# Three changes of queue order in the feed-forward part of a hybrid encoder block

## The chip, the cores and the metric

The kernel runs on one core of a Trainium2 chip. The metric is the device time of one execution in microseconds (us); the median of several executions is compared. A core has a matrix engine (TensorE, PE in the profile), a vector engine (VectorE, DVE), an activation engine (ScalarE, ACT), a general engine (GpSimd, POOL) and a sync engine (SyncE, SP) that here only issues transfers. Each engine works through its own queue of instructions in order, and engines wait for each other by semaphores. Transfers between DRAM and the on-chip memory (DMA) are issued from the queues of SP, ACT or POOL.

## The reference

One residual layer on 2048 rows of 1024 float32 values. Attention and a recurrent mixer come first; the change lies in the last line, the feed-forward network (FFN):

```python
x = x + rms_norm(merged @ w_out, post_mix_g)
hf = rms_norm(x, pre_ffn_g)
u = square(relu(hf @ w_up)) @ w_down      # 1024 -> 4096 -> 1024
x = x + rms_norm(u, post_ffn_g)
```

Every product is to float32 accuracy: each operand is split into a high part (rounded to the matrix engine's float32r) and a low part (operand minus high part), and three matmuls high·high, low·high and high·low are summed.

## The kernel before

**Stages.** The rows are four groups of 512. The mixing of each group comes first (up to about 2050 us of the span) and isn't touched. The FFN then runs over two halves of two groups (1024 rows): `phase_up(0)`, `phase_down(0)`, `phase_up(1)`, `phase_down(1)`. Each of the two products of the FFN is done by a Strassen-Winograd scheme: seven block products in place of eight, on sums and differences of operand blocks.

**Splitting.** `split` (L69) casts to the high part on ACT (L70) and subtracts on DVE to get the low part (L71). A product can begin when the high parts are there and goes on to the low parts one matmul later.

**phase_up.** It runs 16 turns `i`. A turn loads two row blocks of `w_up` (`raw0`, `raw1`, four buffers, L1211), forms the sums `s12` and `s4` on DVE (L1260 to L1266), casts A11/A12 (tile `a1`), S1/S2 (`s12`), S3/A22 (`s3`) and S4 (`s4`), and TensorE runs products with the tiles t2, t3, t1, b22 and t4. The results go through add, relu and square (`hidden`, L1222 to L1224) into the tile X, and from there by GpSimd's DMA to DRAM (`xd`, L1227). For the first eight turns (`early`) the product with `a1` was done ahead, in a loop at the start of the phase, while the operands t2 to t4 were still loading; so only turns 8 to 15 cast `a1` within the turn (L1257). `b1` (tiles bh and bl, "first half" of the activations) is loaded and split by `first_half` (L1161), with `split_here` (L1156), a split in place; for half 1 this is done during `phase_down(0)`, as part of the generator `beside`.

**phase_down.** Seven products, named "1", "6", "7", "5", "4", "3" and "2" in the order in which they run, of eight steps `f` each. A step takes a block of the activations (`xraw`, L1322) and one of `w_down` or its combinations (`wdraw`, L1325 or L1327), each split into the tile `fop`, and runs 24 matmuls, six for each of four row tiles. The loads share four buffers, so the load of one step's block goes out when a low half two steps earlier is done. After a product's last step `gather` adds each row tile's bank into `u` (L1360). After "4" the four tiles of the second group are complete, after "2" those of the first; `final` (L1362) closes a tile: sums of squares on ACT (L1371), multiplication by the gain on DVE (L1372), statistics on GpSimd (L1374, L107), `u * r + x` on DVE (L1378), with `x` loaded by SP into one of two buffers (x1r, L1366), and the store to the output by SP (L1381).

**What sets the order.** The code is written in one order; a scheduler then places each engine's instructions by its own estimate of when their inputs are ready, and the engines keep the order that it made. `queue_behind(a, b)` (L84) adds a dependence without a semaphore, which only tells the scheduler that instruction `a` stands later than `b`. `queue_behind(self.relu, high)` in `operands` (L1331) is one that was there.

Of the kernel before, what the change touches and what calls it, by code (L numbers as in the profile page):

```python
# [24 lines left out]
G = 512  # L25
# [17 lines left out]
def advance(steps, n=None):  # L43

    while n is None or n > 0:
        if next(steps, steps) is steps:
            return
        n = n and n - 1


class Block:
# [1103 lines left out]

    def split_here(self, hi, lo):  # L1156

        self.nc.scalar.copy(hi, lo.bitcast(F32))
        self.nc.vector.tensor_tensor(lo, lo.bitcast(F32), hi.bitcast(F32), ALU.subtract)

    def first_half(self, g, bp):  # L1161

        bh, bl = self.b1 = [bp.tile([P, KB, G], F32R, tag="b" + x, name="b" + x) for x in "hl"]
        for k in range(0, KB, 2):
            ks = slice(k, k + 2)
            self.nc.sync.dma_start(bl[:, ks].bitcast(F32), self.ht[g][:, ks])
            self.split_here(bh[:, ks], bl[:, ks])
            yield

    def phase_up(self, half, zp, rp, cb, pn, early):  # L1170
# [6 lines left out]
        with ExitStack() as ctx:  # L1177
# [36 lines left out]
            def parts(src, tag, n):  # L1214
                pool = sp if tag in ("a1", "s12") else late
                hl = [pool.tile([P, n, P], F32R, tag=tag + x, name=tag + x) for x in "hl"]
                self.split(*hl, src)
                return [[x[:, i : i + KH] for x in hl] for i in range(0, n, KH)]

            def hidden(dst, src, x):  # L1220
# [29 lines left out]
            for i in range(FF // P // 2):  # L1250
                raw0, raw1 = load(2 * i), load(2 * i + 1)
                if i < early:
                    x = cb.tile([P, G], F32, tag="c", name="x11")
                    nc.sync.dma_start(x, self.xd[0][i // 2][:, i % 2])
                (a11, a12), (a21, a22) = ((x[:, lo4], x[:, hi4]) for x in (raw0, raw1))
                if i >= early:
                    A11, A12 = parts(raw0, "a1", KB)  # L1257
                s12 = up.tile([P, KB, P], F32, tag="s1", name="s12")
                s4 = up.tile([P, KH, P], F32, tag="s4", name="s4")
                nc.vector.tensor_tensor(s12[:, lo4], a21, a22, ALU.add)  # L1260
                nc.vector.tensor_tensor(s12[:, hi4], s12[:, lo4], a11, ALU.subtract)
                S1, S2 = parts(s12, "s12", KB)

                nc.vector.tensor_tensor(a21, a11, a21, ALU.subtract)
                S3, A22 = parts(raw1, "s3", KB)
                nc.vector.tensor_tensor(s4, a12, s12[:, hi4], ALU.subtract)  # L1266
                (S4,) = parts(s4, "s4", KH)

                if i < early:
                    p1 = z[:, i]  # L1270
                else:
                    p1 = up.tile([P, G], F32, tag="p1", name="p1")
                    nc.scalar.copy(p1, product(A11, B11, self.pd, "d"))
                    x = first(i, p1)
                q = up.tile([P, G], F32, tag="q", name="q")
                w = up.tile([P, G], F32, tag="w", name="w")
                nc.vector.tensor_tensor(q, p1, product(S2, T["t2"], pn, "dn"), ALU.add)
                if last is not None:
                    sums(*last)
                nc.vector.tensor_tensor(w, q, product(S3, T["t3"], pn, "dn"), ALU.add)  # L1280
                ps = product(S1, T["t1"], pn, "dn")
                hidden(X[:, 1], w, ps)
                keep(2, i, X[:, 1])
                nc.vector.tensor_tensor(q, q, ps, ALU.add)
                hidden(X[:, 2], q, product(S4, T["b22"], pn, "dn"))
                hidden(X[:, 0], w, product(A22, T["t4"], pn, "dn"))
                keep(1, i, X[:, 0])
                last = i, x
            sums(*last)

    def phase_down(self, half, zp, rp, cb, pn, beside_of):
# [4 lines left out]
        with ExitStack() as ctx:  # L1296
# [21 lines left out]
            def operands(s):  # L1318
                q, x, w, f = steps[s]
                t = (zp, ring)[s % 2].tile([P, 4, 2, G], F32R, tag=("z", "op")[s % 2], name="fop")  # L1320
                xr = rp.tile([P, 2, G], F32, tag="raw", name="xraw")
                nc.sync.dma_start(xr, self.xd[x][f])  # L1322
                wr = rp.tile([P, 2, G], F32, tag="raw", name="wdraw")
                if isinstance(w, int):
                    nc.sync.dma_start(wr, self.wd[w][f])  # L1325
                else:
                    nc.sync.dma_start(wr, wrows[w[0]][:, 2 * f : 2 * f + 2, w[1]])  # L1327
                self.split(t[:, 0], t[:, 1], xr)
                high = self.split(t[:, 2], t[:, 3], wr)
                if s == 1:  # L1330
                    self.queue_behind(self.relu, high)  # L1331
                return t

            def bank():
# [27 lines left out]
            def final(t):  # L1362
                th = t // GT
                g, ts = gs[th], slice((t % GT) * P, (t % GT + 1) * P)
                x = op.tile([P, D], F32, tag="x", name="x1r")
                nc.sync.dma_start(x, self.x1[g][ts])  # L1366
                ssq = op.tile([P, 2], F32, tag="ssq", bufs=4, name="ssqu")
                for n in (1, 0):
                    ns = slice(n * G, (n + 1) * G)
                    sq = cb.tile([P, G], F32, tag="c", name="squ")  # L1370
                    nc.scalar.activation(sq, u[t][:, ns], AF.Square, accum_out=ssq[:, n : n + 1])  # L1371
                    nc.vector.tensor_tensor(u[t][:, ns], u[t][:, ns], gt[:, ns], ALU.mult)  # L1372
                    yield
                nc.gpsimd.tensor_tensor(ssq[:, 0:1], ssq[:, 0:1], ssq[:, 1:2], ALU.add)  # L1374
                r = self.rstd(op, ssq[:, 0:1], 1.0 / D, RMS_EPS)
                for n in range(2):
                    ns = slice(n * G, (n + 1) * G)
                    nc.vector.scalar_tensor_tensor(  # L1378
                        u[t][:, ns], u[t][:, ns], r, x[:, ns], op0=ALU.mult, op1=ALU.add
                    )  # L1380
                nc.sync.dma_start(self.out[g * G + ts.start : g * G + ts.stop], u[t])  # L1381
                yield

            NS = len(steps)
# [3 lines left out]
            for s, (q, x, w, f) in enumerate(steps):  # L1388
# [12 lines left out]
                for t in range(GT):  # L1401
                    down(ps[t], t, o, f == 0, f == NF // 4 - 1)
                    if f == NF // 4 - 1:
                        gather(q, t, ps[t])
                        if q == "4":
                            advance(ends[GT + t])
                        elif q == "3":
                            advance(ends[t], 1)
                        elif q == "2":
                            advance(ends[t])  # L1410
                if f % 3 == 1 or f == NF // 4 - 1:
                    advance(beside, 1)
            advance(beside)
# [95 lines left out]
```

## Time and profile before

| | us |
|---|---|
| median of 3 executions (lowest to highest) | 3300.28 (3299.59 to 3302.99) |
| the profiled execution | 3302.74 |
| its span, first to last instruction | 3301.0 |
| TensorE busy / DVE / ACT / POOL | 3189.4 / 2245.6 / 1570.8 / 595.8 |
| phase_up(0), about | 2050 to 2361 |
| phase_down(0), about | 2361 to 2673 |
| phase_up(1), about | 2673 to 2985 |
| phase_down(1), about | 2985 to 3290 |

The profile is of one execution. A timeline row gives the start, the length, the engine, the line and operation, what is written and read, how many such instructions are merged in the row, and in brackets how long the engine stood idle before it and what ended that wait. A row of the list of waits gives the waiting engine and line, what it waited for, and then the total in us, the count and the longest. In a group row the number after the bar is the busy time in us, then the mean length in ns, then the idle time before. In a row of a table by windows the columns are start and end, length, busy us (and count) of PE, PEld (the weight loads), DVE, ACT and POOL, then the granted TensorE clock (1.00 is full), the DMA engines' busy share and GB/s. Successive matmuls overlap: a row's length is longer than the distance between starts. SPq rows are the issue of a DMA, not its transfer.

### The profile page before, as it was taken

The page shows a single profiled execution, that of the slowest core. Times are in us where ns is not written, and L with a number is a line of the kernel's source. Part 1 is how long each engine was busy: PE and PEld are TensorE (multiplying, and loading weights), DVE is VectorE, ACT ScalarE, POOL GpSimd, SP SyncE. Part 2 cuts the span into 40 slices and gives each one's busy share as a digit, 9 for nine tenths or more (in the row PEclk, how much of TensorE's full clock was granted, in tenths as well). Part 3 has the DMA queues.
Part 4 walks back from the last instruction along what each step waited for, and adds up shares of the span by engine and source line. Part 5 has one row for each costly group of instructions (what it writes and reads, how often), then busy time and mean ns, then how long its engine had stood idle before and what let it go on. Part 6 is the DMA issues. An engine that isn't in the chain of part 4 may idle for free. (4 is left out here: it accounts for less than half of the span.)

```text
span 3301.0 us, 49967 instructions
## 1 busy us (share of the span) xinstructions
PE 3189.4 (97%) x18913; PEld 2601.3 (79%) x18913; DVE 2245.6 (68%) x3655; ACT 1570.8 (48%) x2511; POOL 595.8 (18%) x1093
## 2 busy tenths in 40 slices
PE   7999999999999999999999999999999999999998
PEld 5777778778877777878777887878788878888887
DVE  5875766785766875776876775777656667775455
ACT  3434634434744434754444654544543454454343
POOL 2222012222102222111232110122211112220000
PEclk9999999999999999999999999999999999999999
DMA  5335473247564236555326647654787875546665
GB/s 152 90 110 185 129 239 118 81 131 240 170 223 150 87 108 222 189 194 185 96 76 201 200 155 234 231 179 153 248 291 239 285 248 190 170 161 235 193 215 178
DMA packets 432281, 592.53 MB, mean 179 GB/s; under 512 B 25300, under 2 KB 295840, under 8 KB 432040
## 3 DMA queue, kind: packets, MB, share of 16 engines
q1 hardware_dynamic: 375080, 413.14, 40.0%
q0 software_dynamic: 47744, 159.42, 13.1%
q10 hardware_dynamic: 9216, 16.78, 1.4%
q8 instruction: 149, 2.44, 0.3%
q14 instruction: 92, 0.75, 0.1%
HBM read 425.37 MB, written 167.01 MB: 179 GB/s over the span
## 5 line engine op out<-in xcount | busy, mean ns | idle before, releaser
L1345 PE MATMUL ps_dn<-fop 128*128 128x512 f32 x2688 | 611.8, 389 | 2.9 <-DVE fop L71 2.9
L1345 PEld LDWEIGHTS ps_dn<-fop 128*128 128x128 f32 x2688 | 503.9, 188 | 108.9 <-DVE fop L71 4.3
L80 PE MATMUL psd<-hh,whi 128*128 128x512 f32 x1344 | 541.4, 403 | 10.7 <-ACT whi L70 7.0
L80 PE MATMUL psd<-hl,whi 128*128 128x512 f32 x1344 | 542.4, 404 | 0.0
L80 PE MATMUL psd<-hh,wlo 128*128 128x512 f32 x1344 | 538.5, 401 | 2.6 <-DVE wlo L71 2.6
L70 ACT CAST whi<-wraw 128x1024 fp32r<-128x1024 f32 x232 | 243.3, 1049 | 424.1 <-PE psd L80 329.9
L71 DVE TENSOR_TENSOR wlo<-wraw,whi 128x1024 fp32r<-128x1024 f32 x232 | 282.9, 1220 | 165.9 <-ACT whi L70 139.1
L80 PEld LDWEIGHTS psd<-hh,whi 128*128 128x128 f32 x1344 | 255.9, 190 | 62.1 <-ACT whi L70 7.9
L80 PEld LDWEIGHTS psd<-hh,wlo 128*128 128x128 f32 x1344 | 256.1, 191 | 55.9 <-DVE wlo L71 5.1
L80 PEld LDWEIGHTS psd<-hl,whi 128*128 128x128 f32 x1344 | 256.5, 191 | 48.9
L71 DVE TENSOR_TENSOR fop<-xraw,fop 128x1024 fp32r<-128x1024 f32 x112 | 137.0, 1223 | 166.7 <-ACT fop L70 165.9
L70 ACT CAST fop<-xraw 128x1024 fp32r<-128x1024 f32 x112 | 117.8, 1052 | 244.9 <-PE ps_dn L1345 178.5
L1227 POOL DMA_DIRECT2D xd<-X x192 | 103.8, 541 | 394.3 <-ACT X L1224 339.5
L71 DVE TENSOR_TENSOR fop<-wdraw,fop 128x1024 fp32r<-128x1024 f32 x112 | 136.6, 1220 | 26.6 <-ACT fop L70 26.1
L70 ACT CAST fop<-wdraw 128x1024 fp32r<-128x1024 f32 x112 | 117.7, 1051 | 42.8 <-DMA wdraw<-in_w_down_dram 29.8
L903 DVE CUSTOM_DVE_ANT_0 sc<-bias,ps_s 128x640 f32<-128x640 f32 (+4 forms) x128 | 93.8, 732 | 54.0 <-PE ps_pt L914 32.2
L908 ACT ACTIVATE sc<-sc,mn 128x640 f32<-128x640 f32 (+4 forms) x128 | 97.7, 764 | 45.2 <-DVE mn L903 44.8
L70 ACT CAST s12h<-s 128x1024 fp32r<-128x1024 f32 x32 | 33.7, 1054 | 165.0 <-PE ps_u L80 165.0
L80 PE MATMUL ps_p<-yh,whi 128*128 128x512 f32 x256 | 101.3, 405 | 7.5 <-DVE th L1041 3.8
L1070 PE MATMUL ps_o<-whi,mh 128*128 128x512 f32 x256 | 101.6, 397 | 6.1 <-DVE o L1081 6.1
L919 DVE TENSOR_TENSOR PTl<-ps_pt,PTh 128x640 fp32r<-128x640 f32 (+4 forms) x128 | 94.2, 736 | 18.7 <-ACT PTh L918 17.2
L1070 PE MATMUL ps_o<-wlo,mh 128*128 128x512 f32 x256 | 100.6, 393 | 3.2 <-DVE wlo L71 3.2
(368 smaller groups left out, 6826.1 us busy)
## 6 DMA issues: line engine op xcount, KB each, us to landing
wraw<-in_w_in_dram SPq DMA_DIRECT2D x168, 512.0 KB
xraw<-xd SPq DMA_DIRECT2D x112, 512.0 KB
xd<-X POOLq DMA_DIRECT2D x192, 256.0 KB, 5.2
wraw<-in_w_up_dram SPq DMA_DIRECT2D x80, 512.0 KB
wdraw<-wd SPq DMA_DIRECT2D x64, 512.0 KB
wdraw<-in_w_down_dram SPq DMA_DIRECT2D x48, 512.0 KB
gd<-gate ACTq DMA_DIRECT2D x64, 256.0 KB
wd<-cmb POOLq DMA_DIRECT2D x64, 256.0 KB, 3.7
```

What stands on the lines that cost most here:

```text
L70: high = self.nc.scalar.copy(hi, src)
L71: self.nc.vector.tensor_tensor(lo, src, hi.bitcast(F32), ALU.subtract)
L80: mm.append(nc.tensor.matmul(ps, l, r, start=n == 0, stop=n == last).ins)
L903: nc.vector.tensor_tensor_reduce(sc[:, 0:n], bias[:, s0:640], pss[:, c0 : c0 + n], 1.0, 3.0e38, ALU.add, ALU.min, mn,)
L908: nc.scalar.activation(sc[:, 0:n], sc[:, 0:n], AF.Exp, scale=-1.0, bias=mn, accum_out=sm[:, col : col + 1])
L919: nc.vector.tensor_tensor(lv, pst[:, 0:nk], hv.bitcast(F32), ALU.subtract)
L1070: nc.tensor.matmul(ps[t], l[:, k, ts], r[:, k % 2], start=k == 0 and j == 0, stop=k == KB - 1 and j == 2)
L1227: nc.gpsimd.dma_start(self.xd[q][i // 2][:, i % 2], src)
L1345: nc.tensor.matmul(ps, o[:, l, k, sl], o[:, r, k], start=start and n == 0, stop=stop and n == end)
```

## The change

There are three parts.

1. **Casts that need late rows.** In turn 8, the first whose `a1` is cast within the turn, that cast is queued behind the cast of `s3` of turn 7 (`self.cast3`). And the four casts of bh for half 1 are queued behind `self.second`, the cast of the second `fop` operand of `phase_down(0)`.
2. **Closing tiles.** The four tiles that are complete after product "4" are no longer closed right at its last step, all four, but one each at the steps 0 to 3 of product "3", the sixth.
3. **Stores.** In half 0 the eight output tiles are stored from GpSimd's queue, in half 1 from SP's as before.

```diff
     def split_here(self, hi, lo):
-        self.nc.scalar.copy(hi, lo.bitcast(F32))
+        high = self.nc.scalar.copy(hi, lo.bitcast(F32))
         self.nc.vector.tensor_tensor(lo, lo.bitcast(F32), hi.bitcast(F32), ALU.subtract)
+        return high.ins
...
-            self.split_here(bh[:, ks], bl[:, ks])
+            high = self.split_here(bh[:, ks], bl[:, ks])
+            if g:
+                self.queue_behind(high, self.second)
...
-                self.split(*hl, src)
+                self.cast = self.split(*hl, src)
...
                 if i >= early:
+                    behind = self.cast3
                     A11, A12 = parts(raw0, "a1", KB)
+                    if i == early:
+                        self.queue_behind(self.cast, behind)
...
                 S3, A22 = parts(raw1, "s3", KB)
+                self.cast3 = self.cast
...
                 if s == 1:
                     self.queue_behind(self.relu, high)
+                    self.second = high
...
-                nc.sync.dma_start(self.out[g * G + ts.start : g * G + ts.stop], u[t])
+                queue = nc.sync if half else nc.gpsimd
+                queue.dma_start(self.out[g * G + ts.start : g * G + ts.stop], u[t])
...
-                        if q == "4":
-                            advance(ends[GT + t])
-                        elif q == "3":
+                        if q == "3":
                             advance(ends[t], 1)
                         elif q == "2":
                             advance(ends[t])
+                if q == "3" and f < GT:
+                    advance(ends[GT + f])
```

The scheduler turns this into new orders on ACT, DVE, POOL and SP; TensorE's order stays as it was. Three places follow, with the lines of the changed file where the order is the changed one (L1226 and L1227 there are L1223 and L1224 before, L1368 is L1360, L1380 is L1372, L1386 is L1378).

ACT in `phase_up`, turns 6 to 7, before: the cast of `a1` of turn 8 stands right behind the cast of `s12` of turn 6 (X is the tile of the activations).

```order
L70 CAST s12h<-s_21412 128x1024
L70 CAST a1h<-wraw 128x1024
L1223 ACTIVATE X<-X 128x512
L1224 ACTIVATE X<-X 128x512
L70 CAST s4h<-s_21413 128x512
L1223 ACTIVATE X<-X 128x512
L1224 ACTIVATE X<-X 128x512
L70 CAST s3h<-wraw 128x1024
```

And now, from the cast of `s12` of turn 7 on:

```order
L70 CAST s12h<-s_21525 128x1024
L1226 ACTIVATE X<-X 128x512
L1227 ACTIVATE X<-X 128x512
L70 CAST s4h<-s_21526 128x512
L1226 ACTIVATE X<-X 128x512
L1227 ACTIVATE X<-X 128x512
L70 CAST s3h<-wraw 128x1024
L70 CAST a1h<-wraw 128x1024
```

The cast of `a1` has moved by more than one turn, behind the `s3` of turn 7. The same holds in half 1.

ACT at the change from `phase_up(0)` to `phase_down(0)`, before: the four casts of bh stand ahead of the last block's activations and of the casts of the second operand (`fop`).

```order
L1158 CAST bh<-bl 128x1024 x4
L1223 ACTIVATE X<-X 128x512
L1224 ACTIVATE X<-X 128x512
L1223 ACTIVATE X<-X 128x512
L1224 ACTIVATE X<-X 128x512
L70 CAST fop<-xraw 128x1024
L70 CAST fop<-wdraw 128x1024
```

Now:

```order
L1226 ACTIVATE X<-X 128x512
L1227 ACTIVATE X<-X 128x512
L1226 ACTIVATE X<-X 128x512
L1227 ACTIVATE X<-X 128x512
L70 CAST fop<-xraw 128x1024
L70 CAST fop<-wdraw 128x1024
L1226 ACTIVATE X<-X 128x512
L1158 CAST bh<-bl 128x1024
L1227 ACTIVATE X<-X 128x512
L1158 CAST bh<-bl 128x1024
```

The four casts stand behind the second operand's; the other two follow among the casts of the third and fourth operand. DVE's low halves move in the same way. On SP the load of x1r for a closing tile now stands ahead of the loads of operand 4, and a load of xr ahead of half of operand 6's (operands counted from 0).

DVE at the end of product "4" in half 0, before (tiles u_22847 to u_22850 are the four that close; `fop` are the low halves of the steps of product "3"):

```order
L1372 TENSOR_TENSOR u_22849<-u_22849,g_post_24178 128x512 x2
L1378 SCALAR_TENSOR_TENSOR u_22849<-u_22849,rs_r,x1r 128x512 x2
L1360 TENSOR_TENSOR u_22850<-u_22850,ps_dn 128x512
L1372 TENSOR_TENSOR u_22850<-u_22850,g_post_24178 128x512
L71 TENSOR_TENSOR fop<-xraw,fop 128x1024
L1372 TENSOR_TENSOR u_22850<-u_22850,g_post_24178 128x512
L1378 SCALAR_TENSOR_TENSOR u_22850<-u_22850,rs_r,x1r 128x512 x2
L71 TENSOR_TENSOR fop<-wdraw,fop 128x1024
```

Now:

```order
L1386 SCALAR_TENSOR_TENSOR u_22848<-u_22848,rs_r,x1r 128x512 x2
L1368 TENSOR_TENSOR u_22850<-u_22850,ps_dn 128x512
L71 TENSOR_TENSOR fop<-xraw,fop 128x1024
L71 TENSOR_TENSOR fop<-wdraw,fop 128x1024
L71 TENSOR_TENSOR fop<-xraw,fop 128x1024
L71 TENSOR_TENSOR fop<-wdraw,fop 128x1024
L1121 TENSOR_TENSOR cmb<-cmb 128x512
L1380 TENSOR_TENSOR u_22849<-u_22849,g_post_24178 128x512
```

Four low halves, those of steps 2 and 3, now stand ahead of the last steps of the third and fourth tile. SP's loads for steps 4 and 5 no longer stand behind stores, which GpSimd now issues: there each store stands behind its own tile's last step on DVE and ahead of a later tile's statistics.

## The prediction

> **What bounds the kernel now.** I read the page first, then the list of who waited for whom, TensorE (PE) alone, from 1800 us on, since everything up to there is left as it was, then the timelines around each wait.
>
> ```profile
> span 3301.0 us, 49967 instructions
> PE 3189.4 (97%) x18913; PEld 2601.3 (79%) x18913; DVE 2245.6 (68%) x3655; ACT 1570.8 (48%) x2511; POOL 595.8 (18%) x1093
> PE ps_u L80 <- ACT s3h L70: 3.9, 2, 2.1
> PE ps_dn L1345 <- DVE fop L71: 2.9, 3, 1.3
> ```
>
> PE is the bound: 97% of the span. Its order isn't changed, so the change can only close gaps between its matmuls or open new ones. The list names five such gaps (two and three) in the FFN, and all five lie where an edit acts. I measure a gap by when the next matmul starts against when it would have: matmuls of one stream start 0.2267 us apart (from the first row of part B, (5.83 − 0.39) / 24).
>
> **A. The cast of a1 that needs late rows (once in each half).** TensorE's timeline at the first gap, then ScalarE's (ACT), in half 0:
>
> ```profile
> 2179.07 0.39 PE L80 MATMUL ps_u<-t2h,s12l 128*128 128x512 f32 x1
> 2181.60 0.50 PE L80 MATMUL ps_u<-t3h,s3h 128*128 128x512 f32 x1 [2.14 <-ACT s3h L70]
> 2186.60 0.39 PE L80 MATMUL ps_u<-t1h,s12h 128*128 128x512 f32 x1
> ```
> ```profile
> 2171.11 1.06 ACT L70 CAST s12h<-s 128x1024 fp32r<-128x1024 f32 x1 [5.90 <-PE ps_u L80]
> 2176.38 1.05 ACT L70 CAST a1h<-wraw 128x1024 fp32r<-128x1024 f32 x1 [4.21 <-DMA wraw<-in_w_up_dram]
> 2180.51 1.03 ACT L70 CAST s3h<-wraw 128x1024 fp32r<-128x1024 f32 x1
> 2189.31 1.05 ACT L70 CAST s12h<-s 128x1024 fp32r<-128x1024 f32 x1 [6.57 <-PE ps_u L80]
> 2194.75 1.06 ACT L70 CAST s3h<-wraw 128x1024 fp32r<-128x1024 f32 x1
> 2211.29 0.59 ACT L1273 COPY p<-ps_u 128x512 f32<-128x512 f32 x1 [0.68 <-PE ps_u L80]
> ```
>
> The cast of a1 stands behind that of s12 and waits 4.21 us for rows still in flight; s4 and s3 stand behind it. In the next turn, which has no a1, s3 follows s12 by 5.44 us (2194.75 − 2189.31); here by 9.40. With a1 gone from there s3 starts at 2171.11 + 5.44 = 2176.55, and TensorE wants it at 2179.30. The first matmul behind the twelve of t3 should start at 2179.07 + 13 × 0.2267 = 2182.02 and starts at 2186.60: **4.58 us** come off. At its new place, behind the s3 that ends at 2195.8, a1 has 12 us: the product that it feeds ended at 2211.29, so began about 2208.5. Its low half moves along on VectorE (DVE), 1.22 us there in an engine that is idle for 32% of the span; at worst these 1.22 us are paid once in each half.
>
> What is late next? The sums that VectorE forms from the following rows, L1260, which now stand ahead of s4's and s3's low halves. One group tells how late they run over all 32 turns:
>
> ```profile
> L1260 DVE TENSOR_TENSOR s<-wraw 128x512 f32<-128x512 f32 x32 | 22.1, 690 | 2.0 <-DMA wraw<-in_w_up_dram 1.1
> 2180.00:2186.00 6.00, 3.86 (x10) 2.80 (x11) 5.83 (x9) 2.71 (x4) 2.64 (x5) 0.72 0.44 132
> 2804.97 0.39 PE L80 MATMUL ps_u<-t2h,s12l 128*128 128x512 f32 x1
> 2807.09 0.50 PE L80 MATMUL ps_u<-t3h,s3h 128*128 128x512 f32 x1 [1.73 <-ACT s3h L70]
> 2810.77 0.39 PE L80 MATMUL ps_u<-t1h,s12h 128*128 128x512 f32 x1
> ```
>
> 2.0 us in all, so nothing there. In half 1 the same sum is 2810.77 − (2804.97 + 13 × 0.2267) = **2.85 us**. Half 0 loses 1.73 us more because the granted clock was 0.72 from 2180 to 2186 (the window's row); half 1 had full clock behind a gap almost as long, so I take those 1.73 us to come in some executions and not in others. The Trainium skill (TensorE: Matmul & The Clock Gate, Part 1) says that the clock halves after an idle window of about 3.4 us that runs freely, so that the same kernel may or may not be caught. By it no gap of 2.1 us need be caught, and A would be 5.70 in place of 7.43; the trace shows one caught, and the other not.
>
> **B. The casts of bh for half 1.** TensorE, then ScalarE, VectorE and SyncE (SP), at the start of half 0's down phase; then the DMA engines' busy tenths from 2340 to 2400, in slices of 1.5 us, and two groups for the length of one activation and one add (mean ns, before the second bar):
>
> ```profile
> 2360.69 5.83 PE L1345 MATMUL ps_dn<-fop 128*128 128x512 f32 x25
> 2367.78 11.29 PE L1345 MATMUL ps_dn<-fop 128*128 128x512 f32 x48 [1.26 <-DVE fop L71]
> 2379.83 10.97 PE L1345 MATMUL ps_dn<-fop 128*128 128x512 f32 x47 [0.76 <-DVE fop L71]
> ```
> ```profile
> 2357.63 1.05 ACT L1158 CAST bh<-bl 128x1024 fp32r<-128x1024 f32 x1 [0.21 <-DMA bl<-ht]
> 2374.32 1.05 ACT L70 CAST fop<-xraw 128x1024 fp32r<-128x1024 f32 x1 [5.99 <-DMA xraw<-xd]
> 2366.51 1.22 DVE L71 TENSOR_TENSOR fop<-wdraw,fop 128x1024 fp32r<-128x1024 f32 x1
> 2383.34 1.22 DVE L71 TENSOR_TENSOR fop<-wdraw,fop 128x1024 fp32r<-128x1024 f32 x1 [0.76 <-ACT fop L70]
> 2366.61 0.32 SPq L1322 DMA_DIRECT2D xraw<-xd  x1
> DMA  3075899999800059679999999999998968999689
> L1224 ACT ACTIVATE X<-X 128x512 f32<-128x512 f32 x96 | 60.8, 633 | 3.1
> L1238 DVE TENSOR_TENSOR X<-X 128x512 f32<-128x512 f32 x64 | 43.8, 684 | 4.4 <-ACT X L1224 4.2
> ```
>
> TensorE should have gone on at 2360.69 + 25 × 0.2267 = 2366.36: 1.42 lost. Then at 2367.78 + 48 × 0.2267 = 2378.66: 1.17 lost. The four casts wait for bl until 2358.7, and the last block's activations and the second operand's casts stand behind them. Without them those casts hang on TensorE's last products. The last but one has its last start 13 × 0.2267 before 2360.69, and a tail of 0.39: it ends at 2358.1. One add (0.68) and two activations (0.63 each) take it to 2360.1, two casts (1.05) to 2362.2; VectorE meanwhile does four adds to 2362.8 and two low halves (1.22) to 2365.3, in time for 2366.36. So the first loss goes whole.
>
> The second is of another kind: operand 3's load goes out at 2366.61, when operand 1's low half frees its buffer, and its cast waits 5.99 us for it. The load now goes out about 2.8 us earlier; TensorE arrives 2.59 earlier. It is gone if the transfers move along, and stays, together with the first, if the DMA is the limit (ready at 2379.83 either way). The DMA stood empty from 2358 to 2362, so they can mostly move; against it, the load of x1r now stands ahead of operand 4's, and that of xr ahead of half of operand 6's. Ends: 2.59, and −1.0 (the first rival); I take **2.0**, nearer to the end that the empty slices speak for. bh itself is needed 300 us later: nothing. Two of its low halves and an add now lie between operand 1's and 2's on VectorE: operand 2 is ready at 2365.3 + 4 × 1.22 + 0.68 = 2370.9 and wanted at 2366.36 + 24 × 0.2267 = 2371.8. If that cover is gone, what is missing of 0.9 us is paid once.
>
> **C. Closing tiles spread over the sixth product's steps.** TensorE around that product in half 0, and in half 1; VectorE in half 0:
>
> ```profile
> 2559.67 36.20 PE L1345 MATMUL ps_dn<-fop 128*128 128x512 f32 x159
> 2596.81 43.38 PE L1345 MATMUL ps_dn<-fop 128*128 128x512 f32 x190 [0.93 <-DVE fop L71]
> 3149.75 140.01 PE L1345 MATMUL ps_dn<-fop 128*128 128x512 f32 x617
> 2595.53 1.22 DVE L71 TENSOR_TENSOR fop<-wdraw,fop 128x1024 fp32r<-128x1024 f32 x1
> ```
>
> In half 0 one gap: 2596.81 − (2559.67 + 159 × 0.2267) = **1.09 us**, for a low half at 2595.53, queued behind the fourth tile's close. In the new order the low halves of two steps stand right behind the fourth tile's last add, ahead of the third and fourth tile's closes (1.42 us each for their last step alone, L1378 in part D's row), so the one that is late by 1.09 us comes at least 2.8 us earlier and the gap goes. Half 1 has no gap (617 matmuls in one piece): 0. The two closes now stand between the low halves of steps 4, 5 and 6, at least 1.42 us in two steps of 5.4 us each (24 × 0.2267); the rest of each step is the cover, and without it a step would pay these 1.42 us.
>
> **D. First half's stores on GpSimd (POOL).** Eight stores leave SP. The nearest rows are GpSimd's own 512 KB stores (L1445), and the wait that SP's late loads cause at half 1's start:
>
> ```profile
> L1445 POOL DMA_DIRECT2D od<-o x16: 531/534/612, 518.0 to 2051.5; - x16
> 2682.26 0.39 SPq L1211 DMA_DIRECT2D wraw<-in_w_up_dram  x1
> 2681.02 1.22 DVE L71 TENSOR_TENSOR s3l<-wraw,s3h 128x1024 fp32r<-128x1024 f32 x1
> 2690.86 0.50 PE L80 MATMUL ps_u<-bh,a1h 128*128 128x512 f32 x1 [1.25 <-ACT z L1244]
> 2668.11 1.42 DVE L1378 SCALAR_TENSOR_TENSOR u<-u,rs_r,x1r 128x512 f32<-128x512 f32 x2 [1.01 <-POOL rs_r L107]
> 2670.96 0.70 POOL L1374 TENSOR_TENSOR ssqu<-ssqu 128x1 f32<-128x1 f32 x1 [2.88 <-ACT squ L1371]
> ```
>
> Eight times 0.534 is 4.3 us of an engine that is 18% busy. The wait at 2690.86 looks like the gain, but the weight load at 2682.26, ahead of the t loads, waits for s3's low half (2681.02 + 1.22), not for the stores. So **0**; at most the 1.4 us of that wait if s3 moves. The new wait: a store waits for its tile's last VectorE step and holds the next tile's statistics behind it in GpSimd's queue. In the closing tiles that step ends at 2669.53 and the next statistics start at 2670.96: 1.43 us of room against 0.534.
>
> **Sum.** 4.58 + 2.85 + 2.0 + 1.09 = 10.5 us. The profiled execution took 3302.74 us (span 3301.0), so 3292.2 by its own time. It lies 2.46 above the median of the runs, 3300.28: from there 3289.8 if the runs also had the slow clock stretch, 3291.5 if not. I say 3290.5.
>
> **Rivals.**
> - *The DMA takes B back.* The loads don't move, and x1r's 0.5 MB (about 1.7 us at the 311 GB/s below) comes ahead of operand 4, ready 0.7 us ahead of time before (2384.56 against 2385.27): −1.0 in place of 2.0, so about 3293.5. For it: the DMA share.
> ```profile
> 2360.00:2392.00 32.00, 29.99 (x135) 24.16 (x134) 20.32 (x20) 18.46 (x21) 10.29 (x17) 1.00 0.90 311
> ```
> - *A trades one wait for another.* VectorE's L1260 finds its rows as late as a1 did, and half of A comes back: about 3295 to 3297. Against it: 2.0 us in 32 turns.
> - *GpSimd's queue becomes the bound: slower.* If a store holds GpSimd for H us, each of the two stores between closing tiles delays all behind it by H − 1.43, down to s3, the t loads and the gap at 2690.86: 2 × (H − 1.43) us. It outweighs A and B (9.4 us; C is then taken back as well) from H = 6.2; at H = 8 the time is about 3304, at 10 about 3308. Against it: 531 to 612 ns in sixteen cases. The Trainium skill (SBUF — State Buffer, two separate sides) has a rule against this edit: a GpSimd DMA's descriptors can't be written while VectorE holds the shared port, some 0.6 us becoming 3.1; by that figure, an estimate, 2 × 1.67 = 3.3 us come back: about 3294. No GpSimd store here shows it.
>
> **How the numbers follow.** Forecast 0.70 (3288 to 3293), DMA 0.13 (half of it below the mark), A's trade 0.11, GpSimd 0.06 (0.04 of it beyond the mark). A measurement of this kernel can tell about 0.2%, 6.6 us, from no change, so faster means below 3293.7: 0.70 + 0.07 = 0.77; slower means above 3306.9: 0.04; the rest, 0.19, is the same. Range: below, 3290.5 less B whole (0.6), the 1.4 of D and 1.5 for the spread of the runs (3299.59 to 3302.99): 3287; above, the DMA rival and the greater part of A's trade: 3296.
>
> **What would show it.** Right: no wait for s3h at PE; matmul records in one piece over the first 96 of half 0's down phase and over its sixth product; stores on GpSimd of about 0.55 us; the wait near 2690, some 8 us earlier in the span, still there. Wrong: a gap before the s3 products from L1260; operand 3 or 4 waiting for DMA; statistics (L1374) late behind a store.

## The result and the profile after

The changed kernel took 3293.61 us (median of 12 executions, 3290.13 to 3298.61), the kernel before 3303.34 beside it (12 executions, 3299.13 to 3310.88): a ratio of 0.9971, with a 95% interval of 0.9962 to 0.998, so 9.7 us less. Measured again beside other kernels it took 3291.04 against 3302.24: 0.9963 (0.9952 to 0.9975). One execution of a kernel further down (g_post and x1r held) took 11015 us; that kernel's median is of its other five.

The page of its profiled execution (3291.34 us), and TensorE's timeline at the places that the prediction spoke of. The first row is a mark that recurs in every kernel here: the first matmul with t2 in turn 0 of half 0, ahead of everything that differs. Then half 0's down phase, its sixth product, and the start of half 1:

```profile
span 3289.6 us, 49976 instructions
...
PE 3181.5 (97%) x18913; PEld 2599.1 (79%) x18913; DVE 2245.5 (68%) x3655; ACT 1570.2 (48%) x2511; POOL 604.0 (18%) x1101
```
```profile
2092.21 0.50 PE L80 MATMUL ps_u<-t2h,s12h 128*128 128x512 f32 x1 [0.91 <-ACT s12h L70]
...
2353.47 16.48 PE L1353 MATMUL ps_dn<-fop 128*128 128x512 f32 x72
2371.26 0.50 PE L1353 MATMUL ps_dn<-fop 128*128 128x512 f32 x1 [1.31 <-ACT fop L70]
2372.52 11.04 PE L1353 MATMUL ps_dn<-fop 128*128 128x512 f32 x47 [0.76 <-DVE fop L71]
...
2539.74 70.43 PE L1353 MATMUL ps_dn<-fop 128*128 128x512 f32 x310
...
2682.70 0.50 PE L80 MATMUL ps_u<-bh,a1h 128*128 128x512 f32 x1 [1.52 <-ACT z L1247]
```

The mark in the kernel before:

```profile
2094.84 0.50 PE L80 MATMUL ps_u<-t2h,s12h 128*128 128x512 f32 x1 [0.91 <-ACT s12h L70]
```

The mark comes 2.63 us earlier although nothing ahead of it was changed. In the fourteen executions profiled for this document it lies anywhere from 2089.4 to 2096.0 us. So a profile is best read from the mark on: the rest of the FFN took 3301.0 − 2094.84 = 1206.2 us before and 3289.6 − 2092.21 = 1197.4 after, 8.8 us less.

In TensorE's rows the down phase now runs 72 matmuls without a break, so operand 1 is in time, but operand 3 isn't: the 74th matmul should have started at 2353.47 + 73 × 0.2267 = 2370.02 and starts at 2372.52, 2.50 us late. That is what both gaps together cost before (2379.83 − 2360.69 − 16.55 = 2.59). The sixth product is one piece. The wait near 2690 is there, 8 us earlier, as forecast.

ScalarE at the casts of a1, then at operand 3; TensorE in the window in which the clock had fallen to 0.72; SyncE's loads at the start of the down phase; GpSimd at one store between closing tiles, and all stores as a group (ns minimum, median, maximum):

```profile
2168.48 1.05 ACT L70 CAST s12h<-s 128x1024 fp32r<-128x1024 f32 x1 [5.89 <-PE ps_u L80]
...
2173.92 1.05 ACT L70 CAST s3h<-wraw 128x1024 fp32r<-128x1024 f32 x1
...
2187.52 1.05 ACT L70 CAST s3h<-wraw 128x1024 fp32r<-128x1024 f32 x1
2188.48 1.05 ACT L70 CAST a1h<-wraw 128x1024 fp32r<-128x1024 f32 x1
...
2368.05 1.05 ACT L70 CAST fop<-xraw 128x1024 fp32r<-128x1024 f32 x1 [5.98 <-DMA xraw<-xd]
2370.16 1.04 ACT L70 CAST fop<-wdraw 128x1024 fp32r<-128x1024 f32 x1 [1.06 <-DMA wdraw<-in_w_down_dram]
```
```profile
2180.00:2186.00 6.00, 6.00 (x29) 1.00 0.99 325
```
```profile
2353.43 0.33 SPq L116 DMA_DIRECT2D g_post<-in_post_ffn_g_dram  x1
2354.95 0.32 SPq L1090 DMA_DIRECT2D o_prev<-od  x1
2355.36 0.44 SPq L1092 DMA_DIRECT2D xr<-in_x_dram  x1
2356.65 0.32 SPq L1329 DMA_DIRECT2D xraw<-xd  x1
2357.79 0.38 SPq L1334 DMA_DIRECT2D wdraw<-in_w_down_dram  x1
2358.27 0.74 SPq L1374 DMA_DIRECT2D x1r<-x  x1
```
```profile
2661.33 0.62 POOL L1390 DMA_DIRECT2D out_dram<-u  x1 [1.75 <-DVE u L1386]
2662.48 0.69 POOL L1382 TENSOR_TENSOR ssqu<-ssqu 128x1 f32<-128x1 f32 x1 [0.53 <-ACT squ L1379]
...
L1390 POOL DMA_DIRECT2D out_dram<-u x8: 531/620/627, 2576.1 to 2672.3; - x8
```

s3 follows s12 by 5.44 us, a1 stands behind the next s3 and waits for nothing, and TensorE is busy all through 2180 to 2186 at full clock. The store is done before the next statistics could begin: these wait 0.53 us for ScalarE's sum of squares, not for the store. At operand 3 the load (xraw) is issued 3.18 us after the start of the phase (5.92 before), but its cast begins 14.58 us after the start (13.63 before: 2374.32 − 2360.69). In this execution the load left earlier and landed no earlier.

### The profile page after: what moved, and what is told of

It is laid out like the page before. It is cut to its first block, busy times and chain, and to the rows that moved or that the text cites. A ratio compares the mean times of both kernels' runs of the same rounds, so it can differ in the third digit from the quotient of the medians.

```text
span 3289.6 us, 49976 instructions
## 1 busy us (share of the span) xinstructions
PE 3181.5 (97%) x18913; PEld 2599.1 (79%) x18913; DVE 2245.5 (68%) x3655; ACT 1570.2 (48%) x2511; POOL 604.0 (18%) x1101
## 5 line engine op out<-in xcount | busy, mean ns | idle before, releaser
L919 DVE TENSOR_TENSOR PTl<-ps_pt,PTh 128x640 fp32r<-128x640 f32 (+4 forms) x128 | 94.3, 737 | 18.6 <-ACT PTh L918 17.1
```

The lines of the kernel that those rows point to most:

```text
L919: nc.vector.tensor_tensor(lv, pst[:, 0:nk], hv.bitcast(F32), ALU.subtract)
```

## The experiments

Theory: the gain is A, 7.4 us and more where the clock would have fallen, plus C's 1.1; B gives almost nothing, since the transfers issued at the start of the down phase decide when operand 3's rows land; D is nothing. Rivals: A only trades its waits and B and C give the gain; the loads move along and something else in the combined kernel took B; GpSimd's stores cost, or relieve SyncE.

Effects of 1 to 3 us are less than an interval of the medians (about ± 3 to 4 us in five rounds), so the rest of the FFN from the mark to the end of the span is read beside them, one execution each:

| kernel | mark | span | rest of FFN | against before |
|---|---|---|---|---|
| before | 2094.84 | 3301.0 | 1206.2 | |
| a1 edit alone | 2092.06 | 3290.2 | 1198.1 | −8.0 |
| bh edit alone | 2094.41 | 3304.1 | 1209.7 | +3.5 |
| closing tiles alone | 2089.40 | 3296.8 | 1207.4 | +1.2 |
| stores alone | 2089.99 | 3296.8 | 1206.8 | +0.7 |
| changed | 2092.21 | 3289.6 | 1197.4 | −8.8 |
| changed, again | 2092.85 | 3289.9 | 1197.1 | −9.1 |
| changed, old closing tiles | 2095.95 | 3294.2 | 1198.3 | −7.9 |
| changed, x1r held | 2094.55 | 3290.7 | 1196.2 | −10.0 |
| changed, g_post held | 2091.80 | 3287.8 | 1196.0 | −10.2 |
| changed, one more load | 2089.77 | 3285.2 | 1195.4 | −10.7 |
| changed, g_post and x1r held | 2092.51 | 3287.4 | 1194.9 | −11.3 |
| changed, residual held too | 2090.94 | 3285.8 | 1194.9 | −11.3 |
| the same, and z first | 2090.35 | 3284.6 | 1194.3 | −11.9 |

### Each part alone, in the kernel before

**The a1 edit.**

```diff
-                self.split(*hl, src)
+                self.cast = self.split(*hl, src)
...
+                    behind = self.cast3
                     A11, A12 = parts(raw0, "a1", KB)
+                    if i == early:
+                        self.queue_behind(self.cast, behind)
...
                 S3, A22 = parts(raw1, "s3", KB)
+                self.cast3 = self.cast
```

> The kernel before with the a1 edit alone (bh's casts, closing tiles and stores as before). Main theory (the gain is A, plus C's 1.1 us, and B gives 0.2): both waits for s3h are gone from TensorE's list, and 5.7 to 7.4 us of the time with them (ratio about 0.998), the lower figure if the kernel before doesn't run its first gap at the slow clock; the gaps at operands 1 and 3 of half 0's down phase (1.42 and 1.17 us) and the one at its sixth product (1.1) are still there. Rival (A trades one wait for another, and what was gained comes from B and C): a new wait before the s3 products of about 2 us in each half, and under 4 us of gain.

Measured: 3293.53 against 3301.93 us, ratio 0.9975 (0.9966 to 0.9984), so −8.3 us; −8.0 in the table. TensorE has no wait for s3h in either half and no new one there. Its down phase still has both gaps:

```profile
2353.31 5.83 PE L1349 MATMUL ps_dn<-fop 128*128 128x512 f32 x25
2360.33 10.95 PE L1349 MATMUL ps_dn<-fop 128*128 128x512 f32 x47 [1.19 <-DVE fop L71]
2371.46 0.50 PE L1349 MATMUL ps_dn<-fop 128*128 128x512 f32 x1 [0.18 <-ACT fop L70]
2372.72 10.99 PE L1349 MATMUL ps_dn<-fop 128*128 128x512 f32 x47 [0.76 <-DVE fop L71]
```

They sum to 2372.72 − 2353.31 − 73 × 0.2267 = 2.86 us. The rival falls: A alone gives nearly the whole gain. One expectation missed: there was no gap at the sixth product, though the closing tiles were the old ones.

**The bh edit.**

```diff
-            self.split_here(bh[:, ks], bl[:, ks])
+            high = self.split_here(bh[:, ks], bl[:, ks])
+            if g:
+                self.queue_behind(high, self.second)
...
                     self.queue_behind(self.relu, high)
+                    self.second = high
```

> The kernel before with the bh edit alone. Main theory (operand 3's rows land when the DMA engines let them): the gap at operand 1 (1.42 us) goes, the one at operand 3 grows from 1.17 to about 2.4 us, and the time changes by 0 to -0.3 us. Rival (the loads move along, and only in the combined kernel something else ate the gain): both gaps go, -2.6 us. The a1 gap near 2181 is still there, 2.85 us if the clock stays full in it, 4.6 if it falls as in the profile before; the one near 2807 as well.

Measured: 3302.50 against 3301.93, ratio 1.0002 (0.9992 to 1.0013). TensorE in half 0's down phase and at the sixth product, and the granted clock (the figure behind PE's count) in 2 us windows behind the a1 gap of half 0, the gap at the sixth product and the a1 gap of half 1:

```profile
2360.23 16.71 PE L1349 MATMUL ps_dn<-fop 128*128 128x512 f32 x73
2377.33 5.76 PE L1349 MATMUL ps_dn<-fop 128*128 128x512 f32 x24 [0.40 <-DVE fop L71]
2384.09 5.54 PE L1349 MATMUL ps_dn<-fop 128*128 128x512 f32 x23 [0.99 <-DVE fop L71]
...
2596.90 13.45 PE L1349 MATMUL ps_dn<-fop 128*128 128x512 f32 x51 [2.21 <-DVE fop L71]
```
```profile
2182.00:2184.00 2.00, 1.62 (x4) 0.50 0.52 153
...
2598.00:2600.00 2.00, 2.00 (x7) 0.59 0.97 268
2600.00:2602.00 2.00, 2.00 (x6) 0.56 0.82 295
...
2810.00:2812.00 2.00, 2.00 (x6) 0.50 0.60 152
```

The gap at operand 1 is gone, as both theories had it. Operand 3 costs 0.55 and operand 4 another 1.16, together 2384.09 − 2360.23 − 97 × 0.2267 = 1.87 us against 2.59 before: B gave 0.7 here. So the loads moved along in part, and operand 4 became late: between the theories, and far from the rival's 2.6. The +3.5 in the table isn't B's: here half 1's a1 gap was caught by the slow clock as well (4.38 us, 2.85 before), the gap at the sixth product was 2.37 (1.09 before), and the clock fell behind that gap too, so that the 335 matmuls from there to the end of the phase took 77.83 us in place of 76.25. These three make 1.53 + 1.28 + 1.58, less B's 0.7: 3.7.

**The closing tiles.**

```diff
-                        if q == "4":
-                            advance(ends[GT + t])
-                        elif q == "3":
+                        if q == "3":
...
+                if q == "3" and f < GT:
+                    advance(ends[GT + f])
```

> The kernel before with the closing tiles' edit alone. Main theory: the gap of 1.09 us at half 0's sixth product goes, no other comes in its place, half 1 unchanged: -1.1 us, which is less than the time can show; the trace decides. Rival (the two closes between the low halves of steps 4 to 6 make one of them late): a new gap of up to 1.4 us there, 0 to +0.3 us. The a1 gaps near 2181 and 2807 are still there, with or without the slow clock.

Measured: 3298.66 against 3301.93, 0.9995 (0.9987 to 1.0004). The sixth product runs in one piece in both halves and no new gap came with it. The +1.2 in the table is the a1 gaps again (5.29 and 4.45 us, both at the slow clock).

**The stores.**

```diff
-                nc.sync.dma_start(self.out[g * G + ts.start : g * G + ts.stop], u[t])
+                queue = nc.sync if half else nc.gpsimd
+                queue.dma_start(self.out[g * G + ts.start : g * G + ts.stop], u[t])
```

> The kernel before with the first half's stores alone moved to GpSimd's queue. Main theory: 0, the eight stores at 0.53 to 0.63 us each, the wait of about 1.4 us near 2690 still there. Rival (GpSimd can't write descriptors while VectorE works, a store holds its queue 3.1 us): stores of about 3 us, the next closing tile's statistics 1.7 us late behind each, +3.3 us. Second rival (the stores had held SP's late loads): the wait near 2690 goes, -1.4 us. The a1 gaps near 2181 and 2807 are still there, with or without the slow clock.

Measured: 3300.69 against 3301.93, 1.0003 (0.9994 to 1.0012). The stores as a group on GpSimd, and TensorE at the start of half 1:

```profile
L1382 POOL DMA_DIRECT2D out_dram<-u x8: 531/620/627, 2578.6 to 2676.3; - x8
```
```profile
2686.69 0.50 PE L80 MATMUL ps_u<-bh,a1h 128*128 128x512 f32 x1 [1.63 <-ACT z L1244]
```

Neither rival holds: no store was held 3 us, and the wait stayed. Again there was no gap at the sixth product with the old closing tiles.

### What holds operand 3

All of these start from the changed kernel. Without any edit:

> The changed kernel once more, beside the next three, for a second trace of the same program. Main theory: -8 to -10 us against the kernel before, TensorE waits for operand 3 of half 0's down phase 1.5 to 2.5 us (operand 1 in time), no gap at the a1 casts in either half. Rival (the loss at operand 3 was one execution's chance, and the loads of the down phase can move along): no gap at operand 3 in this trace.

Measured: 3291.04 us, 0.9963 (0.9952 to 0.9975). Operand 3 cost 2372.16 − 2354.12 − 16.55 = 1.49 us (2.50 in the first profile), the low end of what was expected, and not nothing; no gap at the a1 casts.

Then loads that aren't needed for 200 us were queued later, `self.loads` being the instructions that load `wdraw`, in order, and `self.gload` the one that loads g_post:

```diff
-                nc.sync.dma_start(x, self.x1[g][ts])
+                row = nc.sync.dma_start(x, self.x1[g][ts]).ins
+                if not half:
+                    self.queue_behind(row, self.loads[8])
...
                     gt = self.gain(op, a["post_ffn_g"], "g_post2")
+                    if not half:
+                        self.queue_behind(self.gload.ins, self.loads[8])
```

> The changed kernel with two loads of half 0's down phase (g_post and the first x1r, 0.5 MB each, not needed for 200 us) queued behind the loads of operand 8. Main theory (bytes ahead of operand 3 decide): g_post alone stood ahead of operand 3's loads, so these land 0.5 MB or about 1.5 us earlier, and of the 2.4 us gap at operand 3 about 1 is left; -1.4 us against the changed kernel. Rival (it's not the bytes but the time from the issue, some 11 us for a load that is split off the queue): gap unchanged at 2.4.

And the residual's first two loads as well:

```diff
-            nc.sync.dma_start(o, self.od[g][t])
+            rows = [nc.sync.dma_start(o, self.od[g][t]).ins]
...
+            if g == self.NG - 1 and t == 0:
+                for row in rows:
+                    self.queue_behind(row, self.loads[3])
```

> As the kernel before this one, and the first o_prev and xr of the residual (0.5 MB each) behind the loads of operand 3 as well. Main theory (bytes): 1.5 MB less ahead of operand 3, its loads land 4 us earlier, no gap at operands 1 to 4: -2.4 us against the changed kernel. The residual's first rows then come about 4 us later, of the 7.5 us that they have until TensorE transposes them (rows ready at 2375.8, transposes at 2383.2). Rival (time from the issue): gap unchanged at 2.4. Rival (the wait moves): TensorE waits at the transposes, or at operand 4, whose loads now stand behind the residual's, for 1 to 2 us.

Measured: 3288.77 us, 0.9956 (0.9944 to 0.9968), and 3292.15, 0.9963 (0.9951 to 0.9976), with 3302.24 for the kernel before. TensorE in the down phase, and operand 3's casts, with g_post and x1r held, then with all four held:

```profile
2353.78 27.40 PE L1354 MATMUL ps_dn<-fop 128*128 128x512 f32 x120
...
2364.42 1.05 ACT L70 CAST fop<-xraw 128x1024 fp32r<-128x1024 f32 x1 [3.01 <-DMA xraw<-xd]
...
2367.42 1.05 ACT L70 CAST fop<-wdraw 128x1024 fp32r<-128x1024 f32 x1 [0.89 <-DMA wdraw<-in_w_down_dram]
```
```profile
2352.19 27.37 PE L1357 MATMUL ps_dn<-fop 128*128 128x512 f32 x120
...
2360.79 1.05 ACT L70 CAST fop<-xraw 128x1024 fp32r<-128x1024 f32 x1 [0.95 <-DMA xraw<-xd]
...
2363.33 1.05 ACT L70 CAST fop<-wdraw 128x1024 fp32r<-128x1024 f32 x1 [1.49 <-DMA wdraw<-in_w_down_dram]
```

120 matmuls run in one piece, so all of B's gaps are gone in both; TensorE doesn't wait at the residual's transposes or at operand 4. From the start of the phase the two casts began at 14.58 and 16.69 us in the changed kernel, at 10.64 and 13.64 with two loads held, at 8.60 and 11.14 with four. Nothing but the loads ahead was changed, so "time from the issue" falls: the wait is for the transfers ahead. But of the first two held loads g_post alone had stood ahead, and without it the casts came 4 and 3 us earlier than in that profile of the changed kernel, not 1.5.

Which of the two it was, with one held at a time:

> The changed kernel with g_post alone held back behind operand 8's loads; x1r still follows operand 3's two loads directly. Measured from the start of half 0's down phase, operand 3's two casts began 14.2 to 14.6 and 15.7 to 16.7 us later in the changed kernel, 10.6 and 13.6 with both loads held. Main theory (the bytes ahead count): the same as with both held, 10.6 and 13.6 to within 0.5 us, no gap. Rival (a load behind them in the queue takes part of the transfer rate too): between the two, 12 to 13 and about 15, a gap of 0 to 1 us.

> The changed kernel with x1r alone held back; g_post still goes first. Main theory (the bytes ahead count): no change, casts at 14 to 14.6 and 15.7 to 16.7 us, a gap of 1.4 to 2.4 us at operand 3. Rival (loads behind count as well): 12 to 13 and about 15, a gap of 0 to 1 us.

One execution each, 3289.50 and 3292.43 us (3299.54 for the kernel before). ScalarE and TensorE with g_post held, then ScalarE with x1r held:

```profile
2363.90 1.05 ACT L70 CAST fop<-xraw 128x1024 fp32r<-128x1024 f32 x1 [3.20 <-DMA xraw<-xd]
...
2366.89 1.05 ACT L70 CAST fop<-wdraw 128x1024 fp32r<-128x1024 f32 x1 [0.90 <-DMA wdraw<-in_w_down_dram]
```
```profile
2353.06 22.17 PE L1354 MATMUL ps_dn<-fop 128*128 128x512 f32 x97
2376.27 5.51 PE L1354 MATMUL ps_dn<-fop 128*128 128x512 f32 x23 [1.04 <-DVE fop L71]
```
```profile
2369.76 1.05 ACT L70 CAST fop<-xraw 128x1024 fp32r<-128x1024 f32 x1 [5.37 <-DMA xraw<-xd]
...
2371.51 1.05 ACT L70 CAST fop<-wdraw 128x1024 fp32r<-128x1024 f32 x1 [0.70 <-DMA wdraw<-in_w_down_dram]
```

With g_post held: 10.84 and 13.83 us from the start (2353.06), the same as with both. With x1r held: 13.96 and 15.71 from 2355.80, as in the changed kernel. So no delay of operand 3 by x1r, which stands behind its loads, is to be seen; g_post, ahead of them, delays it. With g_post alone held operand 4 is 2376.27 − 2353.06 − 97 × 0.2267 = 1.22 us late, and in time when x1r is held too: the prediction's first rival named x1r ahead of operand 4 as the price, and here it can be seen, in one execution of each.

Another load in g_post's place:

```diff
+            if not half:
+                nc.sync.dma_start(u[NT - 1], a["x"][:P])
             NS = len(steps)
```

> The changed kernel with one more load of 0.5 MB (rows of x into the tile of the last row tile, which is written over later) at the place of g_post; g_post now goes where x1r went, behind operand 3's loads. Main theory: a plain load of 0.5 MB ahead costs what g_post costs, so nothing changes for operand 3 (14 to 14.6 and 15.7 to 16.7 us, gap 1.4 to 2.4). Rival (g_post, one row spread over 128 partitions, is the slow transfer): casts 3 us earlier, gap gone.

This told nothing of what it was made for. The new load's tile was free sooner than g_post's, so it went out ahead of the phase (which began at 2351.02):

```profile
2348.27 0.33 SPq L1394 DMA_DIRECT2D u<-in_x_dram  x1
```

With nothing in g_post's place and g_post where x1r had been, the casts began at 10.79 and 14.10 us, operand 3 was in time and operand 4 0.81 us late; 3286.94 us. That repeats the run with g_post held. Whether g_post, one row spread over 128 partitions, is a slower transfer than others of its size stays open.

### The closing tiles in the changed kernel

The changed kernel with the closing edit taken back:

> The changed kernel with the closing tiles as in the kernel before. Main theory, as the runs so far read: the gap at half 0's sixth product comes in some executions only (1.1 us in the profile before and 2.4 with the bh edit alone, none with the a1 edit alone or the stores alone), so 0 or 1 to 2.4 us here, and up to that on the time. Rival (the gap was cured by the a1 edit or the stores, and the closing edit does nothing): none here, and no wait of VectorE for x1r.

One execution, 3295.89 us. TensorE in the down phase of half 0, and operand 3's casts:

```profile
2374.66 5.97 PE L1353 MATMUL ps_dn<-fop 128*128 128x512 f32 x24 [0.75 <-DVE fop L71]
2381.66 5.51 PE L1353 MATMUL ps_dn<-fop 128*128 128x512 f32 x23 [1.04 <-DVE fop L71]
...
2592.93 17.30 PE L1353 MATMUL ps_dn<-fop 128*128 128x512 f32 x75 [0.68 <-DVE fop L71]
```
```profile
2369.29 1.05 ACT L70 CAST fop<-xraw 128x1024 fp32r<-128x1024 f32 x1 [3.48 <-DMA xraw<-xd]
2372.30 1.05 ACT L70 CAST fop<-wdraw 128x1024 fp32r<-128x1024 f32 x1 [1.96 <-DMA wdraw<-in_w_down_dram]
```

The gap at the sixth product is back, 0.84 us, with the a1 edit and the stores in place. With the old closing tiles it was 1.09, 0, 2.37, 0 and 0.84 us in five executions, mean 0.9 (without the slow clock behind the longest); with the new ones nothing in nine. The first two rows are B's gaps once more, 2381.66 − 2357.20 − 97 × 0.2267 = 2.47 us. The casts began 12.09 and 15.10 us after the start of the phase, though SyncE's loads stand as in the changed kernel (14.58 and 16.69, and 14.18 and 15.68 the second time): the same order of loads lands up to 2.5 us apart from one execution to another. So what g_post costs can't be read from one pair: 1.3 to 3.9 us at the first cast. On average the second cast, on which TensorE waits, began 15.6 us after the start in four executions with g_post ahead and without bh's casts ahead (16.69, 15.68, 15.10, and 14.74 with bh's edit alone) and 13.9 in the three with g_post behind (13.64, 13.83, 14.10). These 1.7 us are what 0.5 MB takes at the prediction's 311 GB/s, an estimate, and near the 1.5 that the expectation had put on g_post's bytes.

### A version that is ahead of both

The kernel with four loads held, and in half 1's first loop the cast of t2h, which had waited 3.40 us for its rows in the changed kernel, queued behind the copy of z that stood behind it. The loading and splitting of t2 to t4 (`ops`) also starts later, at turn 2, and goes on by two steps a turn:

```diff
-                        self.split_here(h[:, ks], l[:, ks])
+                        high = self.split_here(h[:, ks], l[:, ks])
+                        if half and n == "t2":
+                            self.queue_behind(high, self.zcopy)
...
-                advance(ops, 1 + i % 2)
+                if i > 1:
+                    advance(ops, 2)
```

> As the kernel before this one, and in half 1's first loop the cast of t2h queued behind the copy of z of turn 2, which had waited behind it in ScalarE's queue. Main theory: besides the 2.4 us at operand 3 the gap of 1.7 us near 2682 goes: -4 us against the changed kernel, -13 to -14 against the kernel before. Rival (the t2h cast was only the first of several late ones): TensorE waits for the next z copy or for the t2 to t4 operands instead, and under 0.7 us of the 1.7 are gained.

Measured: 3288.85 us, 0.9961 (0.9949 to 0.9973); 3.1 us less than the changed kernel in the table, of which 0.6 beside the run with four loads held. The 1.68 us at this place became 1.00, the 0.55 two products on went, a new wait of 0.45 came one product on, and another engine ended the waits:

```profile
2680.32 0.50 PE L80 MATMUL ps_u<-bh,a1h 128*128 128x512 f32 x1 [0.84 <-DVE x L1230]
...
2686.65 0.50 PE L80 MATMUL ps_u<-bh,s12h 128*128 128x512 f32 x1 [0.29 <-DVE x L1230]
```

VectorE's add into x now stands behind two low halves of t2. So the rival holds: 0.68 of the 1.7 us was gained at this place, 0.8 of 2.2 in all, and TensorE now waits for VectorE. Its medians, and those of the held kernels, overlap the changed kernel's; that they are ahead rests on the traces.

## Why the prediction was right, step by step

**A** was right in mechanism and in size. It gave 7.43 us between the two profiles, as worked out, and no wait took its place. Over four executions that still had the old order (before, bh alone, closing tiles alone, stores alone) the two gaps together cost 7.43, 8.94, 9.74 and 7.76 us. The spread is mostly the clock: half 0 was caught by it in all four, half 1 in two. So the 1.73 us that the prediction took to come "in some executions and not in others" came in six cases of eight, and A is worth about 8.5 on average. The Trainium skill (TensorE: Matmul & The Clock Gate, Part 1) names an idle window of about 3.4 us as what halves the clock. These gaps are shorter, 1.7 to 2.7 us and 0.7 more after two matmuls, and six of the eight were caught; that the same gap is caught or not (half 1) fits the page's free-running window. The single gap of 2.37 us at the sixth product with bh's edit alone was caught too. Where the page and these traces differ, the traces decide: a gap need not last 3.4 us to cost half the clock.

**B** was the term that was mis-sized: 2.0 forecast, 0.1 measured between the two profiles. Over four executions each the gaps at operands 1 to 4 sum to 2.59, 2.86, 2.91 and 3.41 us with bh's casts ahead, and to 2.50, 1.49, 1.87 and 2.47 without: 0.9 on average. The first loss went whole, as worked out. The step that failed is "The DMA stood empty from 2358 to 2362, so they can mostly move". Operand 3's loads couldn't use that time: they go out 3.2 us after the phase has begun in every kernel with bh's edit, even with g_post, o_prev and xr held back (2355.38, from 2352.19), and in no kernel here did g_post go out earlier than 0.04 us before its start. Nor did the edit move those two loads alone. In the profile before, o_prev went out 4.23 us after the start (2360.69):

```profile
2364.92 0.32 SPq L1090 DMA_DIRECT2D o_prev<-od  x1
```

Now it's 1.48 (2354.95 from 2353.47), and xr and GpSimd's stores of X (before at 3.26 us, now at 0.51) came forward with it; only g_post stayed. So the row of transfers ahead moved along, behind a start that didn't. Operand 3's second cast, on which TensorE waits, began 17.1 us after the start on average over the four executions with bh's casts ahead and 15.6 over the four without: 1.6 us of the 2.7 by which its loads were issued earlier. That the transfers ahead are the limit is shown by the kernels that hold them; how much each of them takes, g_post apart, is not. What can be taken away there is g_post's 0.5 MB, which the prediction hadn't named; x1r, which it had, was the smaller cost and fell on operand 4 (1.22 us with g_post alone held, one execution).

**C** was right: 1.09 forecast, 1.09 between the profiles, 0.9 on average (1.2 with the slow clock behind the 2.37), but it is a gap that comes in three executions of five.

**D** was right at 0. Sixteen stores in two kernels took 531 to 627 ns each, and none held statistics back by more than some 0.2 us (in the changed kernel those at 2576.75 start when a store ends, and the sum that they need was ready at 2576.52). The Trainium skill's rule (SBUF — State Buffer, two separate sides), by which such a DMA grows from some 0.6 to 3.1 us beside a VectorE copy, is told there of operations in a 2-port mode, and didn't bind beside what VectorE did here: the store at 2580.17 took 0.63 us with VectorE at work on a low half all through it.

**The sum.** 10.5 forecast; 7.43 + 0.1 + 1.09 = 8.6 by the terms, 8.8 and 9.1 by the rest of the FFN, 9.7 by the medians. From a median of 3300.28 the prediction went down 9.8 to 3290.5; that 9.7 came out is partly luck, since by the averages A was worth 1.0 more than its term and B 1.1 less. The 3.1 us by which the time itself was missed are those by which the kernel before was slower in the later measurement (3303.34). The stretch ahead of the mark, 2.63 us shorter in the profile after, isn't the change's.

## What to carry to other kernels

A cast that waits for rows in an in-order queue costs all that stands behind it: look for the wait that has two or more ready instructions queued behind it, and move only that. An operand load that is issued earlier lands earlier by as much only if nothing that is issued with it goes ahead of it: list what becomes issuable at the same moment, and send last what is needed last. And before a term of 1 or 2 us is sized from one profile, look whether its gap comes in every execution, and read executions from a mark behind the part that isn't changed.

## What the hardware showed that wasn't expected

- After TensorE gaps of 1.7 to 2.7 us with another of 0.7 two matmuls later, the granted clock fell to about half for some 2 us (bh alone: 0.50 from 2182 to 2184 and from 2810 to 2812) in six cases of eight, and once after a single gap of 2.37 us (bh alone: 0.59 and 0.56 from 2598 to 2602). From the mark to the last matmul no 2 us window of the fourteen traces shows it anywhere else.
- The same loads in the same order, issued at the same distance from the start of the phase, landed up to 2.8 us apart in four executions (operand 3's first cast at 11.81 us with bh's edit alone, and at 12.09, 14.18 and 14.58).
- One of GpSimd's statistics (L1382 at 2583.55 in the changed kernel), 0.2 to 0.7 us at most other places, took 2.98 us, and 2.98 to 3.00 in all eight executions of kernels with the new closing tiles and GpSimd's stores. In each of them it ended about 0.05 us after a row of VectorE operations with two inputs that left no pause (2586.53 and 2586.48 here). TensorE lost nothing by it; that it waited for VectorE is likely from these times and wasn't tested.
